# Experts of a two-layer trunk: small work as a list of jobs, one per weight chunk, and the norm's gains multiplied into h by GpSimd

## The chip, the cores and the metric

One Trainium2 chip, one core. The metric is the device time of one execution in microseconds (us). The kernel before has a median of 1207.54 us over three runs, from 1207.18 to 1208.95.

## The reference, cut to what matters

256 tokens with 1024 features go through two layers. Each has a mixer (convolutions and gated linear attention) and a feed-forward part: dense in the first layer, experts in the second. The change lies in the second layer's experts.

```python
def _moe(h, w_router, w_g, w_u, w_d):
    t = h.reshape(-1, D)
    logits = (t @ w_router).astype(jnp.float32)
    top_v, top_i = lax.top_k(logits, TOP_K)
    top_w = jax.nn.softmax(top_v, axis=-1)
    gates = jnp.sum(jax.nn.one_hot(top_i, N_EXPERTS) * top_w[..., None], axis=1)
    for e in range(N_EXPERTS):
        out = out + gates[:, e:e + 1] * ((silu(t @ w_g[e]) * (t @ w_u[e])) @ w_d[e])

f = _rmsnorm(h, ffn_norm_g[layer])
h = h + _moe(f, moe_w_router[j], moe_w_gate[j], moe_w_up[j], moe_w_down[j])
```

The hidden width is 2816, and all is float32.

## The kernel before

Every matmul runs on a fast float32 format with fewer bits, so each operand is split into a high and a low half. `split` (L122) lets ACT copy the high half r (L123) and lets DVE subtract it from the source to get the low half l (L125); with a per-row factor, DVE scales and subtracts in one operation (L127). A product is three matmuls (`mm3`, L182 to L184).

The weights come in chunks of 1 MB, 128 partitions by 2048. `weights` (L135) loads one over SP's queue into a ring (`w`, `wx`, and while the experts run also `e2` and `gy`), and splits it into `wr` and `wl`, every fourth time into `wrx` and `wlx` of another pool. So four split chunks have room, and a chunk can be split only when TensorE has used up the one four before it.

`moe` (L644) first adds the mixer's result to h (L653), transposes h for the router's logits, and splits h into `xr` and `xl` (`xt`), tokens on the partitions. Router and top 2 follow, and for every token and expert a place in that expert's list. The eight experts, ordered by load, form four pairs. The even expert of a pair has up to 128 tokens, the odd one ("few") up to 64. `marks` (L779) builds one-hot matrices of the places on DVE. `pick` (L792) gathers a pair's tokens, by matmuls of `xr` and `xl` with these, into a PSUM bank `gb` for two feature tiles at a time, and splits the result into `xg`, tile by tile and expert by expert, with the norm's gain of the tile's features as the scale. `factors` (L818) gathers gate and norm per row, `back` (L831) makes the transposed one-hot matrix for the way back.

The work of an expert is six items, each a gate and an up projection (`proj`), a transpose of the activations (`turn`, or `fold` and `unfold` for the few expert) and a down projection (`lower`, `down`). Results are scaled (`scale`, L939) and added to h (`finish`, L947). The order is written out by hand. A loop over j (L982) appends steps and chunks to the list `prog`: item j of the even experts, and with a lag of two that of the odd ones. Router places and limits are one step at j = 1; the next pair's pick comes in two lumps at the last item of a pair, factors and back right behind; `extras` puts in pieces of scale and finish. Then `in_order` issues the list: before chunk k runs on TensorE, the loads and splits of all chunks to k + 3 are issued.

```python
        fetch(AHEAD)
        k = 0
        with in_order():
            for wanted, fn in prog:
                if wanted is None:
                    fn()
                    continue
                fetch(k + 1 + AHEAD)
                fn(*ready[k])
                k += 1
```

TensorE, ACT and DVE each keep the order of that list.

Of the kernel before, what the change touches and what calls it, by code (L numbers as in the profile page):

```python
# [17 lines left out]
P = 128  # L18
# [27 lines left out]
NCONST = K_TRI + 128  # L46


def small_arrays(i):
    import numpy as np  # L50
    c = np.zeros((P, NCONST), np.float32)
    rows = [i[n].reshape(-1, P) for n in ("attn_norm_g", "ffn_norm_g", "sc_conv_w", "cf_conv_b", "cf_ln_g",
                                          "cf_ln_b", "gla_norm_g", "cf_conv_w")]
# [57 lines left out]
def trunk_kernel(ctx: ExitStack, tc: tile.TileContext, x, w_in, w_out, dense_w_gate, dense_w_up, dense_w_down,  # L111
# [115 lines left out]
    def late_consts():  # L227
        nc.gpsimd.dma_start(wa2, decay_w)
        stg = tmp([P, 11 + NL, P], "stg", tag="E", bufs=1)
        nc.gpsimd.dma_start(stg, consts[:, K_M:].rearrange("p (l q) -> p l q", q=P))  # L230
        return stg
# [412 lines left out]
    def moe(l, j, accs):  # L644
        ft = tmp([P, KT, T], "ft", tag="A", bufs=1)
# [4 lines left out]
        for tt in range(TT):  # L650
            for nh in range(2):
                cs = slice(nh * 512, nh * 512 + 512)
                nc.vector.tensor_tensor(h[:, tt, cs], h[:, tt, cs], accs[tt][nh], op=ALU.add)  # L653
                tp = bank([P, 4, P], "tp")
# [3 lines left out]
                last_x = nc.scalar.activation(xr[:, tt, cs], h[:, tt, cs], AF.Copy)  # L658
                low_half = partial(nc.vector.tensor_tensor, xl[:, tt, cs], h[:, tt, cs], xr.bitcast(F32)[:, tt, cs],
# [65 lines left out]
        def places():  # L725
            nb = bank([P, NE], "nb")
            for tt in range(TT):
                nc.tensor.matmul(nb, oner, msk[:, tt], start=(tt == 0), stop=(tt == 1))
            cnt = tmp([P, NE], "cnt", tag="rt_b", bufs=1)
            nc.vector.tensor_copy(cnt, nb)  # L730
            w0 = cmp[:, 0, 0:NE]
            w1 = cmp[:, 1, 0:NE]
            lte = lt.rearrange("p (a b) -> p a b", b=NE)
            mine = cnt[:, :, None].broadcast_to([P, NE, NE])
            nc.vector.tensor_tensor(w0, cnt[:, None, :].broadcast_to([P, NE, NE]), mine, op=ALU.subtract)
            nc.vector.scalar_tensor_tensor(w1, w0, 0.0, lte, op0=ALU.is_equal, op1=ALU.mult)
            nc.vector.scalar_tensor_tensor(w0, w0, 0.0, w1, op0=ALU.is_lt, op1=ALU.add)
            rank = tmp([P, NE], "rank", tag="rt_r", bufs=1)
            nc.vector.tensor_reduce(rank, w0[:, :, 1:NE], axis=AX.X, op=ALU.add)
            nc.vector.memset(rank[:, 0:1], -1.0)  # L740
            to = cmp[:, 1, 0:NE]
            nc.vector.tensor_tensor(to, target[:, :, None].broadcast_to([P, NE, NE]),
                                    rank[:, None, :].broadcast_to([P, NE, NE]), op=ALU.is_equal)
            nc.vector.tensor_tensor(w0, to, iota[:, None, 0:NE].broadcast_to([P, NE, NE]), op=ALU.mult)
            idf = tmp([P, NE], "idf", tag="rt_j", bufs=1)
            nc.vector.tensor_reduce(idf, w0, axis=AX.X, op=ALU.add)
            nc.vector.tensor_scalar(ids, idf, -1.0, None, op0=ALU.add)
            for tt in range(TT):
                for src, dst in ((pos[:, tt], placed[:, tt]), (gr[:, tt, :, 0], gp[:, tt, :, 0])):
                    nc.vector.tensor_tensor(w0, to, src[:, None, :].broadcast_to([P, NE, NE]), op=ALU.mult)  # L750
                    nc.vector.tensor_reduce(dst, w0, axis=AX.X, op=ALU.add)
            nc.vector.tensor_copy(gp[:, :, :, 1], rs[:, :, None].broadcast_to([P, TT, NE]))
            nc.vector.tensor_tensor(folded, ident[:, 0:FEW], ident[:, FEW:P], op=ALU.add)
            return cnt, rank

        def limits(cnt, rank):
            few = tmp([P, NE], "few", tag="rt_k2", bufs=1)
            room = tmp([P, NE], "room", tag="rt_r2", bufs=1)
            nc.vector.tensor_scalar(few, rank, -0.5, None, op0=ALU.is_gt)
            nc.vector.scalar_tensor_tensor(few, rank, 3.5, few, op0=ALU.is_lt, op1=ALU.mult)  # L760
            nc.vector.tensor_scalar(room, few, float(FEW - P), float(P), op0=ALU.mult, op1=ALU.add)
            nc.vector.tensor_tensor(over, pos, room[:, None, :].broadcast_to([P, TT, NE]), op=ALU.subtract)
            nc.vector.tensor_tensor(few, cnt, room, op=ALU.subtract)
            nc.vector.tensor_scalar(few, few, 0.0, None, op0=ALU.max)
            nc.vector.tensor_reduce(nmax, few, axis=AX.X, op=ALU.max)
# [13 lines left out]
        def marks(p, i):  # L779
            oh = X[p][1]  # L780
            src = pos if p == 0 and i == 0 else placed
            for tt in range(TT):
# [60 lines left out]

        def chunk(e, src, n, a, b, fn):
            prog.append(((e, src, n, a, b), fn))

# [100 lines left out]
        def finish(e, tts):  # L947
            pt = X[e // 2][3]
            for tt in tts:
                for nh in range(2):  # L950
# [12 lines left out]
        def lower(it):  # L963
# [8 lines left out]
        later = []  # L972

        def extras():
            if later:
                q = later[0]
                step(*q.pop(0))
                if not q:
                    later.pop(0)

        n_pairs = len(items[0]) + LAG
        for j in range(n_pairs + 2):  # L982
            hv, hv1 = item(0, j), item(0, j - 1)
            lt_, lt1, lt2 = (item(1, j - LAG - d) for d in range(3))
            p = j // 6
# [17 lines left out]
            if j == 1:  # L1003
                step(marks, 0, 1)
                step(pick, 0, P, P + FEW)
            if j % 6 == 5 and p + 1 < NE // 2:
                step(pick, p + 1, 0, P + FEW, (0, 1))
            extras()
            if lt_:
                step(proj(0, *lt_))  # L1010
            if j == 1:
                step(factors, 0, 1)
                step(back, 0)
            if j % 6 == 5 and p + 1 < NE // 2:
# [4 lines left out]
            extras()  # L1019
            lower(hv1)  # L1020
            if hv:
                step(turn, *hv)
            extras()
# [4 lines left out]
            if j % 6 == 4 and p + 1 < NE // 2:  # L1028
                step(space, p + 1)
                step(marks, p + 1, 0)  # L1030
                step(marks, p + 1, 1)
            extras()
        while later:
            extras()
# [33 lines left out]
        def rest():  # L1068
            with tc.For_i(0, NE, 1) as ev:
# [11 lines left out]
                for k4 in range(2):  # L1081
                    b = bank([P, 4, P], "gb2")
                    for i in range(4):
# [7 lines left out]
                        nc.scalar.activation(x2[:, kt], b[:, i], AF.Copy, scale=col(R_FFN + KT * l + kt))  # L1091
# [113 lines left out]
```

## Time and profile before

| what | before |
|---|---|
| median of 3 runs | 1207.54 us |
| profiled execution | 1209.62 us, span 1207.8 us |
| mean granted TensorE clock | 0.969 |
| TensorE (PE) busy | 1144.5 us, 95% |
| VectorE (DVE) busy | 1000.0 us, 83% |
| ScalarE (ACT) busy | 802.7 us, 66% |
| GpSimd (POOL) busy | 20.3 us, 2% |
| moved by DMA | 348.46 MB, mean 288 GB/s |

The span is what the profiler saw of the core; the execution's own time is 1.8 us longer. A busy share counts the time in which an engine had an instruction running. The granted clock is 1.00 at TensorE's full level (2.4 GHz), and 0.5 at the lower one (1.2 GHz). In the rows below, "L801" is line 801 of the kernel before, and names such as xg or gb are the kernel's tiles.

### The profile page before, as it was taken

The numbers are of one execution on the slowest core, as the hardware profiler recorded it, in microseconds if no ns is written. First come the engines' busy times: TensorE is split into PE (matmuls) and PEld (weight loads), VectorE is DVE, ScalarE is ACT, GpSimd is POOL, SyncE is SP. The second block draws the span as 40 slices with busy tenths as digits, with TensorE's granted clock in tenths as the row PEclk, the third lists the DMA queues.
The fourth block names the chain that finished last, engine by engine and source line by source line (L and its number), as shares of the span: only waits on it lengthen the run. The fifth ranks groups of instructions, "written<-read, shape, count | busy, mean of one in ns | idle before, by whom it ended". The sixth has DMA issues, their size and how long they took to land.

```text
span 1207.8 us, 17210 instructions
## 1 busy us (share of the span) xinstructions
PE 1144.5 (95%) x6633; PEld 1000.4 (83%) x6633; DVE 1000.0 (83%) x1097; ACT 802.7 (66%) x833; POOL 20.3 (2%) x31
## 2 busy tenths in 40 slices
PE   7999999999899987999889999989999979999996
PEld 6998999999799875888778888868888868888875
DVE  5987755555589767699879999879999979999996
ACT  5644543444465455588778888778788778788874
POOL 2000000000000100000000000000000000000000
PEclk9999999999999979799989999989999989999998
DMA  9344454454333562798979999969999969999991
GB/s 370 122 159 168 168 188 175 177 205 162 139 123 122 235 272 99 295 383 304 381 286 400 398 424 386 403 258 402 389 424 385 425 241 397 387 423 409 424 398 37
DMA packets 48791, 348.46 MB, mean 288 GB/s; under 512 B 5431, under 2 KB 5431, under 8 KB 6976
## 3 DMA queue, kind: packets, MB, share of 16 engines
q1 hardware_dynamic: 48384, 345.50, 72.7%
q0 software_dynamic: 320, 1.80, 0.4%
q8 instruction: 54, 0.88, 0.3%
q14 instruction: 33, 0.27, 0.1%
HBM read 346.23 MB, written 1.05 MB: 288 GB/s over the span
## 4 chain that ended last, share of the span: by engine, by line
PE 90%; DVE 5%; ACT 2%; issue 2%; DMA 0%; POOL 0%; POOLq 0%; SPq 0%; DVEq 0%; ACTq 0%
PE gu L182 10%; PE gu L184 10%; PE gu L183 10%; PE acc_y L182 6%; PE acc_y L183 6%; PE acc_y L184 6%; PE gu L865 6%; PE gu L866 6%; PE acc_y L934 3%; PE acc_y L935 3%; PE fb L907 3%; DVE wl L125 2%; PE gb L801 2%; PE sbk L441 1%; PE a_ps L189 1%
## 5 line engine op out<-in xcount | busy, mean ns | idle before, releaser
L125 DVE TENSOR_TENSOR wl<-w,wr 128x2048 fp32r<-128x2048 f32 (+2 forms) x267 | 464.6, 1762 | 72.3 <-ACT wr L123 72.0
L123 ACT ACTIVATE wr<-w 128x2048 fp32r<-128x2048 f32 (+2 forms) x267 | 392.3, 1490 | 189.9 <-issue 114.4
L125 DVE TENSOR_TENSOR wl<-wx,wr 128x2048 fp32r<-128x2048 f32 x54 | 122.6, 2284 | 10.1 <-ACT wr L123 10.0
L182 PE MATMUL gu<-wr,xg 128*128 128x512 f32 (+1 forms) x296 | 112.2, 379 | 0.0
L184 PE MATMUL gu<-wr,xg 128*128 128x512 f32 (+1 forms) x296 | 111.2, 376 | 0.0
L183 PE MATMUL gu<-wl,xg 128*128 128x512 f32 (+1 forms) x296 | 111.1, 375 | 0.0
L125 DVE TENSOR_TENSOR wlx<-w,wrx 128x2048 fp32r<-128x2048 f32 x45 | 102.8, 2284 | 7.0 <-ACT wrx L123 7.0
L123 ACT ACTIVATE wr<-wx 128x2048 fp32r<-128x2048 f32 x54 | 102.4, 1911 | 7.3 <-PE gu L184 3.8
L865 PE MATMUL gu<-wr,xg 128*128 128x512 f32 (+1 forms) x288 | 106.9, 378 | 0.0
L866 PE MATMUL gu<-wl,xg 128*128 128x512 f32 (+1 forms) x288 | 105.5, 373 | 0.0
L182 PE MATMUL gu<-f,wr 128*128 128x256 f32 x336 | 95.1, 283 | 0.0
L183 PE MATMUL gu<-f,wr 128*128 128x256 f32 x336 | 95.0, 283 | 0.0
L184 PE MATMUL gu<-f,wl 128*128 128x256 f32 x336 | 95.0, 283 | 0.0
L182 PE MATMUL acc_y<-wr,hr 128*128 128x512 f32 x228 | 93.0, 408 | 0.0
L183 PE MATMUL acc_y<-wl,hr 128*128 128x512 f32 x228 | 92.0, 403 | 0.0
L184 PE MATMUL acc_y<-wr,hl 128*128 128x512 f32 x228 | 91.6, 402 | 0.0
L123 ACT ACTIVATE wrx<-w 128x2048 fp32r<-128x2048 f32 x45 | 86.2, 1917 | 3.5 <-DVE wl L125 1.6
L184 PEld LDWEIGHTS gu<-wr,xg 128*128 128x128 f32 x296 | 56.3, 190 | 10.5
L182 PEld LDWEIGHTS gu<-wr,xg 128*128 128x128 f32 x296 | 56.6, 191 | 10.1
L183 PEld LDWEIGHTS gu<-wl,xg 128*128 128x128 f32 x296 | 56.4, 190 | 10.2
L183 PEld LDWEIGHTS gu<-f,wr 128*128 128x128 f32 x336 | 64.4, 192 | 0.4
L182 PEld LDWEIGHTS gu<-f,wr 128*128 128x128 f32 x336 | 64.4, 192 | 0.4
(339 smaller groups left out, 2438.7 us busy)
## 6 DMA issues: line engine op xcount, KB each, us to landing
w<-in_moe_w_gate_dram SPq DMA_DIRECT2D x64, 1024.0 KB, 7.8
w<-in_moe_w_up_dram SPq DMA_DIRECT2D x60, 1024.0 KB, 7.8
w<-in_moe_w_down_dram SPq DMA_DIRECT2D x59, 1024.0 KB, 7.7
wx<-in_moe_w_down_dram SPq DMA_DIRECT2D x25, 1024.0 KB, 7.9
wx<-in_moe_w_gate_dram SPq DMA_DIRECT2D x24, 1024.0 KB, 7.6
wx<-in_moe_w_up_dram SPq DMA_DIRECT2D x23, 1024.0 KB, 7.4
w<-in_w_in_dram SPq DMA_DIRECT2D x20, 1024.0 KB, 4.7
w<-in_dense_w_gate_dram SPq DMA_DIRECT2D x11, 1024.0 KB, 4.9
```

Source lines behind the costliest of these rows:

```text
L123: i0 = nc.scalar.activation(r, src, AF.Copy, scale=scale)
L125: i1 = nc.vector.tensor_tensor(l, src, r.bitcast(F32), op=ALU.subtract)
L182: nc.tensor.matmul(o, sr, mr, start=start, stop=False)
L183: nc.tensor.matmul(o, sr, ml, start=False, stop=False)
L184: nc.tensor.matmul(o, sl, mr, start=False, stop=stop)
L189: nc.tensor.matmul(o, s[:, kt], m[:, kt], start=(n == 0 and kt == 0), stop=(n == 2 and kt == KT - 1))
L801: nc.tensor.matmul(b[:, i, c0:c1], xs[:, tt, kt * P:(kt + 1) * P], oh[:, tt].rearrange("p a b -> p (a b)")[:, c0:c1], start=(n == 0), stop ...
L865: nc.tensor.matmul(o, xg[:, 2, kt], wr[:, i], start=(kt == 0), stop=False)
L866: nc.tensor.matmul(o, xg[:, 2, kt], wl[:, i], start=False, stop=(kt == KT - 1))
L907: nc.tensor.matmul(b[:, n, i], kept[n][:, i * P:(i + 1) * P], X[e // 2][4], start=True, stop=True)
L934: nc.tensor.matmul(Y[e][nh], hb, wr[:, i, cs], start=first, stop=False)
L935: nc.tensor.matmul(Y[e][nh], hb, wl[:, i, cs], start=False, stop=fin)
```

## The change

- **Jobs.** A list `jobs` holds small tasks; `chunk` takes one from it behind each weight chunk. The router's `places` becomes six functions (count, order, assign, where, shares, limits). marks, factors, back and every pick of two feature tiles are one job each, scale two and finish four. `collect` queues a pair's jobs: pair 1 at j = 4, the others when the odd expert two pairs earlier is through. Before the first item of a new pair, picks that are left are issued at once. `extras` is gone, and the turn of item 0 stands behind the first projection of item 1.
- **Gains.** A row of the norm's gains is added to the constants (K_GAIN). `moe` loads it to all partitions, 128x1024, over POOL's queue; POOL multiplies h by it into `hg`, four times 128x512, and `xr` and `xl` are split from hg. hg shares a tile `fh` with the transposed `ft`.
- **Evictions.** A pick's split takes both feature tiles at once, 128x256 for the even expert and 128x2x64 for the few one, without a scale.

```diff
 def moe(l, j, accs):
-        ft = tmp([P, KT, T], "ft", tag="A", bufs=1)
+        gains = mix.tile([P, D], F32, name="gains")
+        nc.gpsimd.dma_start(gains, bass.AP(tensor=consts.tensor, offset=consts.offset + K_GAIN, ap=[[0, P], [1, D]]))
+        fh = tmp([P, 2, KT * T], "fh", tag="A", bufs=1)
...
                 nc.vector.tensor_tensor(h[:, tt, cs], h[:, tt, cs], accs[tt][nh], op=ALU.add)
+                nc.gpsimd.tensor_tensor(hg[:, tt, cs], h[:, tt, cs], gains[:, cs], op=ALU.mult)
...
-                last_x = nc.scalar.activation(xr[:, tt, cs], h[:, tt, cs], AF.Copy)
-                low_half = partial(nc.vector.tensor_tensor, xl[:, tt, cs], h[:, tt, cs], xr.bitcast(F32)[:, tt, cs],
+                last_x = nc.scalar.activation(xr[:, tt, cs], hg[:, tt, cs], AF.Copy)
+                low_half = partial(nc.vector.tensor_tensor, xl[:, tt, cs], hg[:, tt, cs], xr.bitcast(F32)[:, tt, cs],
...
-                for i in range(2):
-                    kt = 2 * k2 + i
-                    gain = col(R_FFN + KT * l + kt)
-                    if c0 == 0:
-                        split(b[:, i, 0:P], xg[:, 0, kt], xg[:, 1, kt], scale=gain)
-                    if c1 > P:
-                        split(b[:, i, P:P + FEW], xg[:, 2, kt, 0:FEW], xg[:, 2, kt, FEW:P], scale=gain)
+                ks = slice(2 * k2, 2 * k2 + 2)
+                if c0 == 0:
+                    split(b[:, :, 0:P], xg[:, 0, ks], xg[:, 1, ks])
+                if c1 > P:
+                    split(b[:, :, P:P + FEW], xg[:, 2, ks, 0:FEW], xg[:, 2, ks, FEW:P])
...
+        jobs = []
+
         def chunk(e, src, n, a, b, fn):
             prog.append(((e, src, n, a, b), fn))
+            if jobs:
+                step(*jobs.pop(0))
...
-                later.append([(scale, e, (0,)), (scale, e, (1,)), (finish, e, (0,)), (finish, e, (1,))])
+                jobs.extend([(scale, e, (0,)), (scale, e, (1,))])
+                jobs.extend((finish, e, (tt,), (nh,)) for nh in range(2) for tt in range(TT))
+                if e % 2 == 1 and e < NE - 3:
+                    collect(e // 2 + 2)
+
+        def collect(p):
+            jobs.extend([(space, p), (marks, p, 0), (marks, p, 1)])
+            jobs.extend([(factors, p, 0), (factors, p, 1), (back, p)])
+            jobs.extend((pick, p, 0, P + FEW, (k2,)) for k2 in range(KT // 2))
+
+        jobs.extend((fn,) for fn in places())
+        jobs.extend([(marks, 0, 1), (factors, 0, 1), (back, 0)])
+        jobs.extend((pick, 0, P, P + FEW, (k2,)) for k2 in range(KT // 2))
...
+            if j == 4:
+                collect(1)
+            if hv and hv[1] == 0 and j:
+                while any(job[0] is pick for job in jobs):
+                    step(*jobs.pop(0))
...
             if j == 1:
-                step(lambda: limits(*places()))
-            extras()
+                step(turn, *hv1)
...
-                step(pick, p + 1, 0, P + FEW, (0, 1))
...
-                step(pick, p + 1, 0, P + FEW, (2, 3))
-                for i in range(2):
-                    step(factors, p + 1, i)
-                step(back, p + 1)
```

How the order moves is seen on three engines. First DVE behind the first gather. Before, from the turn of item 0 (hl) to the first few-expert gather, with the router's placement (L730 to L765, 27 operations in all) between two weight splits:

```order
L125 TENSOR_TENSOR hl_4609<-tb_4603,hr_4608 128x512
L125 TENSOR_TENSOR wlx_4614<-e2_4411,wrx_4613 128x2048
L125 TENSOR_TENSOR wl_4632<-e2_4411,wr_4631 128x2048
L730 COPY cnt_4652<-nb_4649 128x8
L735 TENSOR_TENSOR cmp_4413<-cnt_4652 128x64
L736 SCALAR_TENSOR_TENSOR cmp_4413<-cmp_4413,kc_73 128x64
L737 SCALAR_TENSOR_TENSOR cmp_4413<-cmp_4413 128x64
L739 TENSOR_REDUCE rank_4657<-cmp_4413 128x8
L740 MEMSET rank_4657 128x1
L742 TENSOR_TENSOR cmp_4413<-kc_73,rank_4657 128x64
L744 TENSOR_TENSOR cmp_4413<-cmp_4413,kc_73 128x64
L746 TENSOR_REDUCE idf_4662<-cmp_4413 128x8
```

The same engine after the change:

```order
L744 COPY cnt_4441<-nb_4543 128x8
L127 TENSOR_TENSOR wl_4550<-w_4547,wr_4549 128x2048
L749 TENSOR_TENSOR cmp_4419<-cnt_4441 128x64
L750 SCALAR_TENSOR_TENSOR cmp_4419<-cmp_4419,kc_73 128x64
L751 SCALAR_TENSOR_TENSOR cmp_4419<-cmp_4419 128x64
L752 TENSOR_REDUCE rank_4442<-cmp_4419 128x8
L753 MEMSET rank_4442 128x1
L843 COPY rg_4573<-rgb_4570 128x2
L127 TENSOR_TENSOR wl_4580<-wx_4577,wr_4579 128x2048
L756 TENSOR_TENSOR cmp_4419<-kc_73,rank_4442 128x64
L758 TENSOR_TENSOR cmp_4419<-cmp_4419,kc_73 128x64
L759 TENSOR_REDUCE idf_4443<-cmp_4419 128x8
```

The placement now begins before the second split of the projections, and a group of it stands behind each split.

Second, ACT at a gather for a whole pair. Before, the first lump of eight evictions (xg) and what follows:

```order
L123 ACTIVATE xg_5444<-gb_5557,kc_73 128x128
L123 ACTIVATE xg_5444<-gb_5557,kc_73 128x64
L123 ACTIVATE xg_5444<-gb_5557,kc_73 128x128
L123 ACTIVATE xg_5444<-gb_5557,kc_73 128x64
L123 ACTIVATE xg_5444<-gb_5574,kc_73 128x128
L123 ACTIVATE xg_5444<-gb_5574,kc_73 128x64
L123 ACTIVATE xg_5444<-gb_5574,kc_73 128x128
L123 ACTIVATE xg_5444<-gb_5574,kc_73 128x64
L123 ACTIVATE wr_5593<-wx_5591 128x2048
L123 ACTIVATE wr_5608<-wx_5606 128x2048
L876 ACTIVATE kept_5620<-gu_5597 128x512
```

After the change, at the third pair:

```order
L125 ACTIVATE wrx_6741<-w_6739 128x2048
L125 ACTIVATE xg_6616<-gb_6758 128x256
L125 ACTIVATE xg_6616<-gb_6758 128x2x64
L125 ACTIVATE wr_6773<-w_6771 128x2048
L125 ACTIVATE xg_6616<-gb_6789 128x256
L125 ACTIVATE xg_6616<-gb_6789 128x2x64
L125 ACTIVATE wr_6805<-wx_6803 128x2048
L125 ACTIVATE xg_6616<-gb_6818 128x256
L125 ACTIVATE xg_6616<-gb_6818 128x2x64
L125 ACTIVATE wr_6833<-wx_6831 128x2048
L125 ACTIVATE xg_6616<-gb_6845 128x256
```

Two evictions stand between two weight copies, four times; DVE has the same pattern with its subtractions.

Third, POOL's queue at the kernel's start, after the change; before, the row L648 is not there:

```order
L350 MEMSET u_133 128x2x30
L230 DMA wa2_79<-in_decay_w_dram 17x512
L648 DMA gains_4337<-in_consts_dram 128x1024
L260 ISA
L260 TENSOR_TENSOR st_88<-st_88,half_75 128x1
```

The load of the gains stands ahead of POOL's first part of the norm (st).

## Rows read from the trace of the kernel before

**Rows 1.** The page: TensorE's busy time, and the chain that ended last by engine.

```profile
PE 1144.5 (95%) x6633; PEld 1000.4 (83%) x6633; DVE 1000.0 (83%) x1097; ACT 802.7 (66%) x833; POOL 20.3 (2%) x31
...
PE 90%; DVE 5%; ACT 2%; issue 2%; DMA 0%; POOL 0%; POOLq 0%; SPq 0%; DVEq 0%; ACTq 0%
```

**Rows 2.** Stretches: us, PE, PEld, DVE, ACT, POOL busy, clock, DMA share, GB/s.

```profile
455.00:500.00 45.00, 34.91 (x149) 29.53 (x148) 28.16 (x52) 20.59 (x21) 0.00 (x0) 0.81 0.43 167
500.00:597.00 97.00, 97.00 (x487) 81.59 (x486) 90.16 (x58) 77.48 (x60) 0.00 (x0) 1.00 0.93 361
597.00:611.00 14.00, 6.46 (x35) 5.76 (x34) 8.65 (x18) 8.57 (x18) 0.00 (x0) 0.65 0.67 265
611.00:780.00 169.00, 169.00 (x839) 141.95 (x838) 161.78 (x108) 137.68 (x108) 0.00 (x0) 1.00 0.96 389
...
604.40:787.30 182.90, 175.27 (x871) 147.56 (x872) 170.43 (x126) 146.15 (x123) 0.00 (x0) 0.98 0.94 379
```

**Rows 3.** Waits of TensorE from 440 us on: us in total, times, longest.

```profile
PE ptb L836 <- DVE xg L127: 11.1, 3, 3.7
PE rgb L823 <- ACT kept L876: 9.3, 3, 3.1
PE gb L801 <- DVE xg L787: 6.7, 1, 6.7
PE tb L895 <- DVE s L886: 3.4, 1, 3.4
...
PE rgb L823 <- DVE xg L127: 2.3, 3, 0.8
```

**Rows 4.** Chain of waits from 455 to 500 us: start, duration, what.

```profile
464.60 1.11 PE tb L895 x4
...
484.73 7.04 PE gb L801 x32
```

**Rows 5.** Chain of waits around the first boundary, from 597 to 613 us.

```profile
597.57 1.78 PE gb L801 x16
...
608.46 1.09 PE ptb L836 x4
609.55 0.43 PE acc_y L182
...
611.57 0.23 PE acc_y L184
```

**Rows 6.** Groups by form from 424 us on: busy, mean ns of one | idle before.

```profile
L125 DVE TENSOR_TENSOR wl<-wx,wr 128x2048 fp32r<-128x2048 f32 x54 | 122.6, 2284 | 10.1 <-ACT wr L123 10.0
...
L125 DVE TENSOR_TENSOR hl<-tb,hr 128x512 fp32r<-128x512 f32 x20 | 13.6, 681 | 1.8 <-ACT hr L123 1.8
...
L127 DVE SCALAR_TENSOR_TENSOR xg<-gb,kc,xg 128x128 fp32r<-128x128 f32 x32 | 11.1, 349 | 8.7 <-ACT xg L123 8.5
L127 DVE SCALAR_TENSOR_TENSOR xg<-gb,kc,xg 128x64 fp32r<-128x64 f32 x32 | 9.1, 284 | 15.1 <-ACT xg L123 15.1
...
L125 DVE TENSOR_TENSOR wl<-w,wr 128x1024 fp32r<-128x1024 f32 x2 | 2.4, 1216 | 0.0
...
L125 DVE TENSOR_TENSOR hl<-tb,hr 128x256 fp32r<-128x256 f32 x4 | 1.7, 416 | 0.0
...
L123 ACT ACTIVATE wr<-wx 128x2048 fp32r<-128x2048 f32 x54 | 102.4, 1911 | 7.3 <-PE gu L184 3.8 <-PE acc_y L184 1.8 <-ACT wrx L123 0.9
```

**Rows 7.** Timeline of ACT and of DVE at that boundary.

```profile
606.23 0.31 ACT L123 ACTIVATE xg<-gb,kc 128x64 fp32r<-128x64 f32 x1 [2.28 <-DVE xg L127]
...
601.44 4.50 DVE L125 TENSOR_TENSOR wl<-wx,wr 128x2048 fp32r<-128x2048 f32 x2 [1.51 <-ACT wr L123]
```

**Rows 8.** Timeline of POOL, DVE and ACT in the first 27 us.

```profile
22.43 1.79 POOL L237 CAST mk<-stg 128x1024 uint8<-128x1024 f32 x1 [9.24 <-DMA stg<-in_consts_dram]
...
22.09 3.20 DVE L125 TENSOR_TENSOR wl<-w,wr 128x1024 fp32r<-128x1024 f32 x2 [2.54 <-ACT wr L123]
...
9.36 2.00 ACT L123 ACTIVATE wr<-w 128x1024 fp32r<-128x1024 f32 x2 [2.20 <-DMA w<-in_w_in_dram]
```

More of the change, by code (lines that the diff above doesn't have):

```diff
@@ L45 @@
 K_TRI = K_ONE + 128
-NCONST = K_TRI + 128
+K_GAIN = K_TRI + 128
+NCONST = K_GAIN + D
 def small_arrays(i):
@@ L51, in small_arrays @@
     c = np.zeros((P, NCONST), np.float32)
+    c[0, K_GAIN:] = i["ffn_norm_g"][1]
     rows = [i[n].reshape(-1, P) for n in ("attn_norm_g", "ffn_norm_g", "sc_conv_w", "cf_conv_b", "cf_ln_g",
@@ L229, in late_consts @@
         stg = tmp([P, 11 + NL, P], "stg", tag="E", bufs=1)
-        nc.gpsimd.dma_start(stg, consts[:, K_M:].rearrange("p (l q) -> p l q", q=P))
+        nc.gpsimd.dma_start(stg, consts[:, K_M:K_GAIN].rearrange("p (l q) -> p l q", q=P))
         return stg
@@ L644, in moe @@
     def moe(l, j, accs):
-        ft = tmp([P, KT, T], "ft", tag="A", bufs=1)
+        gains = mix.tile([P, D], F32, name="gains")
+        nc.gpsimd.dma_start(gains, bass.AP(tensor=consts.tensor, offset=consts.offset + K_GAIN, ap=[[0, P], [1, D]]))
+        fh = tmp([P, 2, KT * T], "fh", tag="A", bufs=1)
+        ft = fh[:, 0].rearrange("p (k t) -> p k t", k=KT)
+        hg = fh[:, 1].rearrange("p (t d) -> p t d", t=TT)
         xt = tmp([P, 2, TT, D], "xt", tag="Y", bufs=1, dt=F32R)
@@ L725, in places @@
         def places():
[L726 to L730, printed above, removed]
+            cnt, rank, idf, few, room = (tmp([P, NE], n, tag="rt_" + n, bufs=1)
+                                         for n in ("cnt", "rank", "idf", "few", "room"))
             w0 = cmp[:, 0, 0:NE]
             w1 = cmp[:, 1, 0:NE]
-            lte = lt.rearrange("p (a b) -> p a b", b=NE)
@@ L734, in places @@
[L734 to L765, printed above, removed]
+            to = cmp[:, 0, NE:2 * NE]
@@ new lines, in places, with count, order @@
+            V = nc.vector
+            def count():
+                nb = bank([P, NE], "nb")
+                for tt in range(TT):
+                    nc.tensor.matmul(nb, oner, msk[:, tt], start=(tt == 0), stop=(tt == 1))
+                V.tensor_copy(cnt, nb)
+            def order():
+                lte = lt.rearrange("p (a b) -> p a b", b=NE)
+                mine = cnt[:, :, None].broadcast_to([P, NE, NE])
+                V.tensor_tensor(w0, cnt[:, None, :].broadcast_to([P, NE, NE]), mine, op=ALU.subtract)
+                V.scalar_tensor_tensor(w1, w0, 0.0, lte, op0=ALU.is_equal, op1=ALU.mult)
+                V.scalar_tensor_tensor(w0, w0, 0.0, w1, op0=ALU.is_lt, op1=ALU.add)
+                V.tensor_reduce(rank, w0[:, :, 1:NE], axis=AX.X, op=ALU.add)
+                V.memset(rank[:, 0:1], -1.0)
@@ new lines, in assign, with move @@
+            def assign():
+                V.tensor_tensor(to, target[:, :, None].broadcast_to([P, NE, NE]),
+                                rank[:, None, :].broadcast_to([P, NE, NE]), op=ALU.is_equal)
+                V.tensor_tensor(w0, to, iota[:, None, 0:NE].broadcast_to([P, NE, NE]), op=ALU.mult)
+                V.tensor_reduce(idf, w0, axis=AX.X, op=ALU.add)
+                V.tensor_scalar(ids, idf, -1.0, None, op0=ALU.add)
+            def move(tt, src, dst):
+                V.tensor_tensor(w0, to, src[:, None, :].broadcast_to([P, NE, NE]), op=ALU.mult)
+                V.tensor_reduce(dst, w0, axis=AX.X, op=ALU.add)
@@ new lines, in where, with shares, limits @@
+            def where():
+                for tt in range(TT):
+                    move(tt, pos[:, tt], placed[:, tt])
+            def shares():
+                for tt in range(TT):
+                    move(tt, gr[:, tt, :, 0], gp[:, tt, :, 0])
+                V.tensor_copy(gp[:, :, :, 1], rs[:, :, None].broadcast_to([P, TT, NE]))
+                V.tensor_tensor(folded, ident[:, 0:FEW], ident[:, FEW:P], op=ALU.add)
+            def limits():
+                V.tensor_scalar(few, rank, -0.5, None, op0=ALU.is_gt)
+                V.scalar_tensor_tensor(few, rank, 3.5, few, op0=ALU.is_lt, op1=ALU.mult)
+                V.tensor_scalar(room, few, float(FEW - P), float(P), op0=ALU.mult, op1=ALU.add)
+                V.tensor_tensor(over, pos, room[:, None, :].broadcast_to([P, TT, NE]), op=ALU.subtract)
+                V.tensor_tensor(few, cnt, room, op=ALU.subtract)
+                V.tensor_scalar(few, few, 0.0, None, op0=ALU.max)
+                V.tensor_reduce(nmax, few, axis=AX.X, op=ALU.max)
@@ L767, in moe @@
+            return count, order, assign, where, shares, limits
         gw, uw, dw = moe_w_gate[j], moe_w_up[j], moe_w_down[j]
@@ L777, in block, with marks @@
             return src[bass.ds(expert[p], 1), n].rearrange("e p n -> (e p) n")
-        def marks(p, i):
+        def marks(p, i, tts=range(TT)):
             oh = X[p][1]
             src = pos if p == 0 and i == 0 else placed
-            for tt in range(TT):
+            for tt in tts:
                 e = 2 * p + i
@@ L945, in scale, with finish @@
             return last
-        def finish(e, tts):
+        def finish(e, tts, nhs=(0, 1)):
             pt = X[e // 2][3]
             for tt in tts:
-                for nh in range(2):
+                for nh in nhs:
                     cb = bank([P, 512], "cb")
@@ L969, in lower @@
             if c == 5 and e < NE - 1:
-                later.append([(scale, e, (0,)), (scale, e, (1,)), (finish, e, (0,)), (finish, e, (1,))])
[L972 to L979, printed above, removed]
+                jobs.extend([(scale, e, (0,)), (scale, e, (1,))])
[9 more added lines that the diff above has]
+        jobs.extend((pick, 0, P, P + FEW, (k2,)) for k2 in range(KT // 2))
         n_pairs = len(items[0]) + LAG
@@ L1002, in moe @@
                 step(proj(1, *hv))
[L1003 to L1006, printed above, removed]
-                step(pick, p + 1, 0, P + FEW, (0, 1))
-            extras()
             if lt_:
                 step(proj(0, *lt_))
[L1011 to L1014, printed above, removed]
-                step(pick, p + 1, 0, P + FEW, (2, 3))
-                for i in range(2):
-                    step(factors, p + 1, i)
-                step(back, p + 1)
-            extras()
             lower(hv1)
-            if hv:
+            if hv and j:
                 step(turn, *hv)
-            extras()
             if lt_:
@@ L1027, in moe @@
                 lower(lt2)
[L1028 to L1034, printed above, removed]
+        for job in jobs:
+            step(*job)
         queue = [q[0] for q in prog if q[0] is not None]
@@ L1090, in rest @@
                                 n += 1
-                        nc.scalar.activation(x2[:, kt], b[:, i], AF.Copy, scale=col(R_FFN + KT * l + kt))
+                        nc.scalar.activation(x2[:, kt], b[:, i], AF.Copy)
                 b = bank([P, T], "ptb2")
```

1 line of the change is left out of this document (removed).

## The prediction

> **What bounds the kernel now.** I began with the page's busy shares and the chain of waits. TensorE is busy 95% of the span and is 90% of the chain that ended last [rows 1], so time is to be had only where TensorE stands still or runs at its lower clock. Next, a table by stretches of the experts' part [rows 2]. From 500 to 597 and from 611 to 780 us TensorE is busy without a gap at the full granted clock (97.00 of 97.00, 169.00 of 169.00): nothing the change does there can show. Two kinds of stretch are different: the **start** of the experts (455 to 500 us: 34.91 of 45 busy, clock 0.81) and a **boundary between two pairs** (597 to 611 us: 6.46 of 14, clock 0.65). The third view, TensorE's waits from 440 us on, says what ended them [rows 3]. At the start the gather of the few expert waits 6.7 us for its one-hot marks and the turn of item 0 waits 3.4 us for DVE's product s, 10.1 us in all. The boundary comes three times, and its waits add up to 11.1 + 9.3 + 2.3 = 22.7 us, 7.6 us each: for an eviction (xg) on DVE, or for a copy (kept) on ACT which stands behind the evictions.
>
> Behind each wait TensorE runs at the 1.2 GHz level for a while. At the start 32 gather matmuls took 7.04 us and the four transposes of item 0 took 1.11 us [rows 4]; in the gap-free stretch ahead of a boundary 16 wider gather matmuls took 1.78 us [rows 5], so 32 should take 3.56. A 512-column matmul takes 0.43 us behind a wait and 0.23 us otherwise [rows 5]; nine of them stand behind the two waits of the start, and at least four behind each boundary.
>
> **The change, part by part.**
>
> *Jobs at the start.* 27 small DVE operations of the router stood in one lump between two weight splits. They now stand in groups of up to seven, one group behind each chunk; the turn of item 0 moves behind item 1's first projection, and the second gather comes in four pieces. No DVE work disappears. What TensorE loses in 455 to 500 us today is 10.1 us of waiting, 3.5 us in the slow gather, half of 1.11 in the slow transposes, and nine matmuls by 0.20 (1.8): about 16 us. Its work without these is 29 us. DVE is busy 28.16 us in the same stretch [rows 2], so it just keeps up, but it has to deliver a split every 2.28 us [rows 6] with the groups between them, each of which TensorE may meet. Following the new order by hand I find waits of 1.0, 0.5 and about 0.5 us left: 31 us in place of 45, a **gain of 14 us**. The bounds: 16 if nothing is left, 3 if the lump only changes into many short waits that keep the clock low. I take 14, because TensorE keeps work in reserve: one chunk's products stand between the marks and the first instruction that needs them, and the gather comes two chunks later still.
>
> *Collections at the boundaries.* Before, sixteen evictions on each engine came in two lumps of eight. Within a lump ACT and DVE take turns, since they go to the same PSUM bank: ACT's next eviction waits for DVE's last one, 2.28 us where DVE still has a split ahead of it [rows 7]. Two splits of DVE, 4.50 us, stand between the lumps [rows 7]. Now one group of two feature tiles is gathered behind each of four chunks, and its evictions are two operations on each engine in place of four. Their price: DVE's 128x128 form with the gain took 0.349 us and its 128x64 form 0.284 [rows 6]; the new 128x256 has a row of its own in hl, 0.416, and for the new 128x2x64 I take the 0.35 of the 128x128 form. DVE per pair: 8 x 0.349 + 8 x 0.284 = 5.1 becomes 4 x (0.416 + 0.35) = 3.1, so 2.0 us less. That by itself is hidden (DVE is busy 170.43 of 182.90 us per pair [rows 2]).
>
> What decides is the cycle. The second eviction on ACT still waits for DVE's first one (one bank). Behind it ACT makes the high half of the next chunk (1.91), then DVE the low half (2.28) [rows 6], then DVE's first eviction (0.42), then ACT's second (0.3): with the hand-overs about 5.1 us per gather chunk. TensorE needs 8 or 12 matmuls by 0.23 and half of 1.78 for the gather: 2.8 to 3.7 us. Four such chunks run late by 6 to 9 us in all. Chunks are split three ahead: at best TensorE has three chunks of some 2.6 us in hand when the first late one takes 1.91 + 2.28, a reserve of up to 3.6 us. So 4 to 7 us are still lost at each boundary, where it is 7.6 us of waiting and about 2 at the low clock now. I take 5.5 lost, a gain of 4 each, **12 us for three**. The bounds are nothing, and all 28.
>
> *Gains multiplied by GpSimd.* POOL takes four products of 128x512 in the chain that ends in the first gather, and ACT's and DVE's halves of x wait for them. No POOL product of that size stands in the trace. The nearest rows: a POOL cast of 128x1024 took 1.79 us [rows 8], twice the elements with one input; DVE's two-input form of the same size, hl of 128x512, took 0.681 [rows 6]. Between them I take 1.2 us. Router and logits do not go through it: they hang on h and its transposes. But ACT's copies for the logits stand in one queue with the halves. Beside the cast, two DVE operations of 128x1024 took 3.20 us [rows 8] where each takes 1.216 [rows 6]: a loss of 0.8 us. Against this, the marks of the first expert now stand ahead of two weight splits on DVE, which saves up to 0.8 us. I take **0.6 us lost**, bounds -0.4 and 2.
>
> The Trainium skill, in SBUF — State Buffer, Who interferes with whom, says that a VectorE instruction with two SBUF inputs and a GpSimd instruction that reads SBUF exclude each other, whichever starts second standing fully blocked. The 3.20 us beside the cast agree with a block. By that rule alone each of the four products could hold a DVE operation for its whole length, 4.8 us in all by my 1.2; I don't take this, since VectorE's row of that stretch also waits for ACT and TensorE, which hides a part.
>
> *Gains loaded at the start.* A new broadcast of 512 KB goes out on POOL's queue in the first microseconds, when the first weight copy on ACT waits 2.20 us for its DMA [rows 8]. At the 389 GB/s of rows 2 it costs at most 1.3 us; at least nothing. I take **0.8 us lost**, as all queues share the same engines. Its place among POOL's instructions has a second effect: later chunks' memory overlaps it, and two loads wait until POOL has read it; TensorE has enough loaded chunks there, so nothing.
>
> The turn of item 0, the finish in four steps and the rest beyond 977 us move within gap-free stretches: nothing.
>
> **Sum.** -14 - 12 + 0.6 + 0.8 = -24.6. The profiled execution took 1209.62 us (span 1207.8), 2.1 above the median 1207.54. So 1185.0 against it, **1183** as a median.
>
> **Rivals.**
>
> 1. *The boundaries vanish wholly* (the reserve covers all four gathers). For it: the evictions are spread over four chunks. Against it: DVE would have 168 of 173 us to work, and the weights' DMA, whose share is 0.94 over a pair at 379 GB/s [rows 2], would need 0.99. 1209.6 - 14 - 28 + 1.4 = 1169, as a median 1167. Chance 0.13.
> 2. *Only one half pays.* Either the evictions at a boundary still take turns with splits between them, and the loss stays 9.5 us: 1209.6 - 14 + 1.4, as a median 1195. Or the start gains only its lower bound, 3: 1209.6 - 3 - 12 + 1.4, as a median 1194. For it: in the new order a weight split now stands between every two evictions, so each of them can be as late as a split is. Chance 0.21.
> 3. *Slower: TensorE fed in pieces drops to 1.2 GHz and stays there.* At a boundary it now gets four pieces of 3 us, one every 5.1 us, where it had two long waits. At the low level a gather chunk takes 5.6 to 7.4 us, more than the 5.1 of its feeders, so TensorE itself becomes the bound; should it stay there for six chunks, it loses about 6 x 2.8 + 3 = 20 us per boundary, 10 more than now. 1209.6 - 14 + 1.4 + 30 = 1227, as a median 1225. It decides if the granted clock over such a stretch falls below about 0.6. Against it: before, the full level was back after four slow matmuls [rows 5]. Chance 0.05.
> 4. *The change does not do what it says*: the jobs run, but the same waits come under other names, and all ends within 0.2% (2.4 us, about what a measurement of this kernel can tell from no change). Chance 0.03.
>
> **How the numbers follow.** The forecast has 0.58. It and rivals 1 and 2 are all faster by more than 0.2%, together 0.92; the same 0.03; slower 0.05. The range goes from a little below rival 1 (both bounds of the start on top of it) to a little above rival 2: 1163 to 1198. What is left out are rivals 3 and 4 and the tails.
>
> **What the next profile would show.** Right: no wait of the gather for marks (6.7) and the gather at the full level; in 455 to 490 us TensorE idle under 3 us; at each boundary several waits of 1 to 2 us for splits or evictions in place of two of 3 to 4, with a granted clock above 0.8; POOL with four products of 1 to 1.5 us near 428 to 436 us; the first weight copy on ACT up to a microsecond later. Wrong: waits of TensorE at the boundaries still over 7 us each (rival 2), a gap-free boundary (rival 1), rows of 0.43 us over a dozen matmuls behind each gather (rival 3), or an end of the router that is more than 2 us later than today, from POOL's products.

## The result and the profile after

The changed kernel takes **1186.52 us** (median of 4 runs, 1185.49 to 1187.54), against 1208.24 for the kernel before: ratio 0.9819, 95% interval 0.9805 to 0.9832. The forecast was 1183, the range 1163 to 1198. So the medians differ by 21.7 us. The profiled execution took 1185.49 us with a span of 1183.5, so 24.1 us less than the one of before; the sum had 24.6. The profile of before fell on a long execution (1209.62 us), this one on the shortest of four, which brings the two figures nearer. "L841" is now line 841 of the kernel after; the kernels of the experiments have lines of their own.

The page of the kernel after, busy times and chain by engine, answers to [rows 1]:

```profile
PE 1138.0 (96%) x6633; PEld 992.4 (84%) x6633; DVE 990.5 (84%) x1065; ACT 789.5 (67%) x801; POOL 28.0 (2%) x36
...
PE 80%; DVE 10%; issue 4%; ACT 4%; DMA 1%; POOL 0%; SPq 0%; POOLq 0%; DVEq 0%; ACTq 0%
```

TensorE runs 6633 matmuls as before. They keep it busy for 6.5 us less (1138.0 for 1144.5), since fewer of them stand at the low level; the rest of the gain is time in which it stood still. DVE's share of the chain doubled from 5 to 10%. That is not more waiting of TensorE, which is busy for 96% of the span and has only 80% of the chain: around a boundary the chain now runs over DVE and ACT while TensorE still works on chunks in hand. The stretches after (columns as in [rows 2]), and one of before that is as wide:

```profile
457.00:490.00 33.00, 28.94 (x134) 23.40 (x133) 27.30 (x44) 19.62 (x16) 0.00 (x0) 0.95 0.64 246
490.00:560.00 70.00, 70.00 (x344) 58.51 (x343) 62.49 (x46) 54.96 (x42) 0.00 (x0) 1.00 0.87 329
560.00:600.00 40.00, 37.66 (x205) 32.35 (x204) 32.16 (x26) 29.50 (x30) 0.00 (x0) 0.96 0.79 298
600.00:740.00 140.00, 140.00 (x686) 117.10 (x685) 136.33 (x94) 113.79 (x89) 0.00 (x0) 1.00 1.01 412
740.00:790.00 50.00, 46.31 (x235) 38.60 (x234) 43.28 (x30) 38.72 (x34) 0.00 (x0) 0.97 0.86 327
930.00:970.00 40.00, 36.27 (x193) 30.08 (x191) 37.66 (x24) 33.93 (x27) 0.00 (x0) 1.00 0.91 359
```

```profile
750.00:800.00 50.00, 42.37 (x230) 36.65 (x229) 41.06 (x44) 34.69 (x39) 0.00 (x0) 0.90 0.80 326
```

At the start the granted clock is 0.95, where it was 0.81. Around the three boundaries it is 0.96, 0.97 and 1.00, where the second one had 0.90 in a stretch of 50 us before. TensorE stands still there for 2.3, 3.7 and 3.7 us, where it was 7.5 of 14 at the first one [rows 2] and 7.6 at the second. The stretches between are gap-free as before. TensorE's waits from 430 us on (us in all, times, longest) answer to [rows 3]:

```profile
PE rgb L841 <- DVE xg L807: 3.6, 1, 3.6
PE gu L888 <- DVE wl L127: 3.3, 3, 1.8
PE acc_y L956 <- DVE hb L127: 2.4, 1, 2.4
PE gu L185 <- DVE wl L127: 2.1, 2, 1.9
PE gu L888 <- DVE wlx L127: 1.8, 1, 1.8
```

The waits for evictions and for kept at the boundaries, 22.7 us in all, are gone. In their place stand waits for weight splits (wl, wlx). One new wait stands in the tail: 2.4 us for hb (the few expert's split activations) of the last item. And 3.6 us for the few expert's marks are left at the start, where the forecast had no more than 1; they now hold up the gather of its factors (rgb), not of its tokens.

How a boundary looks now is read from ACT's and DVE's timelines at the second one:

```profile
745.19 0.37 ACT L125 ACTIVATE xg<-gb 128x256 fp32r<-128x256 f32 x1
747.98 0.28 ACT L125 ACTIVATE xg<-gb 128x128 fp32r<-128x128 f32 x1 [2.42 <-DVE xg L127]
748.33 1.91 ACT L125 ACTIVATE wr<-wx 128x2048 fp32r<-128x2048 f32 x1
750.14 0.37 ACT L125 ACTIVATE xg<-gb 128x256 fp32r<-128x256 f32 x1
...
745.32 2.29 DVE L127 TENSOR_TENSOR wl<-wx,wr 128x2048 fp32r<-128x2048 f32 x1 [0.85 <-ACT wr L125]
747.53 0.41 DVE L127 TENSOR_TENSOR xg<-gb,xg 128x256 fp32r<-128x256 f32 x1
748.29 0.29 DVE L127 TENSOR_TENSOR xg<-gb,xg 128x128 fp32r<-128x128 f32 x1 [0.34 <-ACT xg L125]
750.27 2.29 DVE L127 TENSOR_TENSOR wl<-wx,wr 128x2048 fp32r<-128x2048 f32 x1 [1.69 <-ACT wr L125]
```

This is the cycle of the forecast. ACT's second eviction (747.98) begins 0.04 us after DVE's first one ends (747.94), which stands behind DVE's split; ACT's next weight copy stands behind the eviction, and DVE's next split behind that copy. From one first eviction to the next (745.19 to 750.14) it takes 4.95 us; the forecast had 5.1. The Trainium skill, in PSUM — Partial Sum Buffer, PSUM bank collisions raise a hardware error, states that two engines must not be at one PSUM bank at the same time; the 0.04 us agree with accesses put in series for that.

### The profile page after: what moved, and what is told of

Read it like the earlier page. It is cut to its first block, busy times and chain, and to the rows that moved or that the text cites. A ratio compares the mean times of both kernels' runs of the same rounds, so it can differ in the third digit from the quotient of the medians.

```text
span 1183.5 us, 17163 instructions
## 1 busy us (share of the span) xinstructions
PE 1138.0 (96%) x6633; PEld 992.4 (84%) x6633; DVE 990.5 (84%) x1065; ACT 789.5 (67%) x801; POOL 28.0 (2%) x36
## 4 chain that ended last, share of the span: by engine, by line
PE 80%; DVE 10%; issue 4%; ACT 4%; DMA 1%; POOL 0%; SPq 0%; POOLq 0%; DVEq 0%; ACTq 0%
PE gu L184 9%; PE gu L185 9%; PE gu L186 9%; PE acc_y L184 6%; PE acc_y L185 6%; PE acc_y L186 6%; DVE wl L127 5%; PE gu L888 5%; PE gu L887 5%; PE fb L929 3%; PE acc_y L956 3%; PE acc_y L957 2%; ACT wr L125 2%; DVE wlx L127 2%; PE sbk L443 1%
## 5 line engine op out<-in xcount | busy, mean ns | idle before, releaser
L185 PEld LDWEIGHTS gu<-wl,xg 128*128 128x128 f32 x296 | 57.1, 193 | 12.6 <-DVE wl L127 2.6
L888 PEld LDWEIGHTS gu<-wl,xg 128*128 128x128 f32 x288 | 54.3, 189 | 13.0 <-DVE wl L127 4.3
L185 PEld LDWEIGHTS gu<-f,wr 128*128 128x128 f32 x336 | 64.4, 192 | 0.4
```

Of the source, the lines that this page charges most:

```text
L185: nc.tensor.matmul(o, sr, ml, start=False, stop=False)
L888: nc.tensor.matmul(o, xg[:, 2, kt], wl[:, i], start=False, stop=(kt == KT - 1))
```

## The experiments

Each edit is made alone to the kernel after the change, to be compared with its 1186.52, where nothing else is said. The kernel before, run beside these, had medians from 1208.99 to 1209.73 us, where it had 1208.24 beside the changed one. So a difference of under some 1.5 us is not told apart from none.

**The gains loaded later.** The load waits in POOL's queue behind the last norm of the second mixer.

```diff
-        nc.gpsimd.dma_start(gains, ...)
+        with behind((area["power"],)):
+            nc.gpsimd.dma_start(gains, ...)
```

> The load of the gains goes out behind the last norm of the second mixer (about 320 us) instead of in the first 3 us; all else as after the change. Theory (the 512 KB stand ahead of the first weights on the same DMA engines): the first split of a weight on ACT starts about 2.0 us earlier, at 9.3 in place of 11.4 us, the whole kernel becomes 2 to 3 us faster, 1183.5 to 1184.5, and nothing is given back at 320 us. Rival (the first 440 us are longer for another reason, such as the wider row of constants): first weight copy still near 11.4 us, time 1186 to 1187.

Measured 1182.89 us (1181.74 to 1183.37), 3.6 less. The first weight copy on ACT, in the kernel after and with the late load:

```profile
11.40 2.00 ACT L125 ACTIVATE wr<-w 128x1024 fp32r<-128x1024 f32 x2 [4.08 <-DMA w<-in_w_in_dram]
```

```profile
9.44 2.00 ACT L125 ACTIVATE wr<-w 128x1024 fp32r<-128x1024 f32 x2 [2.24 <-DMA w<-in_w_in_dram]
```

Its wait for the DMA was 2.20 us before the change [rows 8], 4.08 after it, and is 2.24 with the late load. The theory holds: the load cost 2.0 us at once, and in these two traces 2.4 us by the first logit (436.57 against 434.13 us); nothing is given back at 320 us. The 3.6 us of the medians are a little more than was expected.

**ACT's evictions first.** Same instructions, another order.

```diff
-                if c0 == 0:
-                    split(b[:, :, 0:P], xg[:, 0, ks], xg[:, 1, ks])
...
+                for s, r, _ in todo:
+                    nc.scalar.activation(r, s, AF.Copy)
+                for s, r, low in todo:
+                    nc.vector.tensor_tensor(low, s, r.bitcast(F32), op=ALU.subtract)
```

> In a pick's eviction ACT writes both high halves before DVE subtracts either, so that ACT's second eviction no longer waits for DVE's first one (it did for 2.42 us, twice per boundary in the trace after the change). Theory (cycle of weight copy, weight split, eviction on DVE, eviction on ACT, 4.95 us per pick, is what TensorE waits for at the boundaries): cycle falls to some 3.0 us, TensorE's waits at the three boundaries fall from 2.3, 3.7 and 3.6 us to under 1 each, and the time by 6 to 8 us, 1178 to 1180. Rival A (weights' DMA or DVE's own work is the bound there): the waits move to a DMA or stay, gain under 3 us. Rival B (the even and the few expert's evictions contend for the bank): ACT's and DVE's evictions grow longer, no gain.

Measured 1169.94 us (1169.74 to 1172.46): 16.6 less, twice what was expected. ACT's timeline and the stretch of the second boundary:

```profile
739.22 0.55 ACT L832 ACTIVATE xg<-gb 128x256 fp32r<-128x256 f32 x2 [0.39 <-PE gb L821]
739.66 1.92 ACT L125 ACTIVATE wr<-wx 128x2048 fp32r<-128x2048 f32 x1
741.97 0.55 ACT L832 ACTIVATE xg<-gb 128x256 fp32r<-128x256 f32 x2 [0.39 <-PE gb L821]
...
740.00:765.00 25.00, 25.00 (x147) 21.92 (x146) 23.00 (x17) 21.39 (x19) 0.00 (x0) 1.00 0.97 360
```

The two evictions stand together, the cycle is 2.75 us (739.22 to 741.97), and ACT now waits for TensorE's gather. TensorE has no gap at any boundary. Rival A falls: DVE (23.00 of 25 us) and the DMA (0.97) still had room. So does rival B: ACT's two evictions take 0.55 us together, no longer than apart (0.37 and 0.28). The size was off in the main because only the waits were counted, 9.8 us in all. Behind the wait of 1.8 us in the kernel after, the chain has matmuls at the low level:

```profile
757.87 0.79 PE gu L888
758.66 0.43 PE gu L887
...
761.22 0.18 PE gu L184
```

Seven matmuls there took 3.35 us (757.87 to 761.22) in place of 1.6. At the first boundary narrower ones did so, at the third none. The profiled executions differ by 13.0 us; the rest of the 16.6 is not accounted for.

**limits behind the few expert's gather.** The job of seven small DVE operations goes from ahead of the marks to the end of the first list.

> The job limits (7 small DVE operations) goes from ahead of the few expert's marks to the end of the first list. Theory (TensorE's 3.6 us wait for the marks at 476 us is one of order on DVE): marks come 3 to 4 us earlier, the wait vanishes with the matmuls of 0.43 us behind it, 3 to 5 us faster, 1181.5 to 1183.5. Rival (DVE is full there, 27.3 of 33 us, so that another wait for DVE takes its place): gain under 1.5 us, with a new wait for hl or a weight split of 2 us or more in the same place.

Measured 1184.11 us, but from 1180.61 to 1187.25, so its size is unsure. The marks (L807) on DVE in the kernel after, and with the edit:

```profile
477.04 2.28 DVE L127 TENSOR_TENSOR wl<-gy,wr 128x2048 fp32r<-128x2048 f32 x1
479.23 0.48 DVE L807 TENSOR_SCALAR xg<-kc,placed 128x128 fp32r<-128x128 f32 x2
```

```profile
474.45 0.48 DVE L807 TENSOR_SCALAR xg<-kc,placed 128x128 fp32r<-128x128 f32 x2
...
475.44 2.28 DVE L127 TENSOR_TENSOR wl<-gy,wr 128x2048 fp32r<-128x2048 f32 x1
```

The marks come 4.8 us earlier, 0.7 of them by an earlier first gather: neither limits nor that split stands ahead of them now. But with one job fewer in the list their user on TensorE also moved up by one chunk, so the wait fell only from 3.6 to 2.4 us. From the first gather to that of the second pair it takes 115.7 us in place of 118.6: the place itself gained 2.9 us in this trace, near the theory. The profiled execution lost them again behind, where the edit moves nothing, with a mean clock of 0.981 for 0.985. The rival's new wait did not come.

**Additions of expert 6 behind the last hb.**

> The four additions of expert 6's result to h are made behind the last item's hb, their matmuls stay where they are. Theory (spread one behind each of the last weight splits, they hold up s and hb of the last item, for which TensorE waits 2.4 us): hb comes 2 to 2.5 us earlier, the wait falls under 0.5, the time by 1.5 to 2.5 us, 1184 to 1185. Rival (the additions then delay the last yg and the final norm by as much, since DVE has only 2.0 us free there): no change, within 0.5 us of 1186.5.

Measured 1183.55 us (1182.62 to 1185.08), 3.0 less, a little more than expected. The wait for hb fell from 2.4 to 0.5 us, and the four additions find room on DVE just ahead of the last yg (the scaled result):

```profile
1167.05 0.29 DVE L127 TENSOR_TENSOR hb<-s,hb 128x128 fp32r<-128x128 f32 x1 [0.38 <-ACT hb L125]
1167.26 2.47 DVE L973 TENSOR_TENSOR h<-h,cb 128x512 f32<-128x512 f32 x4
1169.65 1.40 DVE L129 SCALAR_TENSOR_TENSOR yg<-acc_y,rg,yg 128x512 fp32r<-128x512 f32 x2
```

**The jobs alone.** Gains, load and two-tile evictions are taken back.

> The jobs alone: POOL's product, the load of the gains and the two-tile evictions are taken back, a pick evicts tile by tile with the gain as scale. Theory (what TensorE waits for at a boundary is a cycle in series over ACT and DVE; four evictions per engine in place of two make it about 1.5 us longer, 6.5 in place of 4.95): each boundary loses some 5 us more, the load's 3.5 us are not paid, 1194 to 1203. Rival (the number of evictions does not matter, they hide behind the splits): 1182 to 1185.

Measured 1206.59 us (1204.40 to 1207.89), ratio to the kernel before 0.9978 (0.9967 to 0.9988). So the jobs by themselves bring almost nothing, less than the theory's range; the rival is far off. ACT at the second boundary:

```profile
754.69 0.36 ACT L125 ACTIVATE xg<-gb,kc 128x128 fp32r<-128x128 f32 x1
757.41 0.32 ACT L125 ACTIVATE xg<-gb,kc 128x64 fp32r<-128x64 f32 x1 [2.37 <-DVE xg L129]
...
760.88 0.36 ACT L125 ACTIVATE xg<-gb,kc 128x128 fp32r<-128x128 f32 x1
```

The cycle is 6.19 us (754.69 to 760.88) in place of 4.95, as four evictions per engine take turns. TensorE's waits at the three boundaries come to 20.7 us, so nearly the 22.7 of before, and the tail has the new wait of 2.4 us for hb. Where the rest of what the start wins is lost was not followed.

**The gains alone**, in the order of the kernel before.

> The other half alone: gains by POOL and two-tile evictions in the order of the kernel before, without jobs. Theory: the start keeps its 10.1 us of waits; at each boundary a lump has four evictions in turn in place of eight, some 2.5 us less each, of which TensorE's waits give back 2 to 4 us per boundary; the load costs 3. Sum 1208 - 9 + 2: 1199 to 1204. Rival (the lumps' length does not matter, only the splits between them): 1208 to 1211, slower than before by the load.

Measured 1199.05 us (1197.48 to 1199.80), ratio 0.9917 (0.9900 to 0.9933): the theory, at its lower end. TensorE's waits from 440 us on:

```profile
PE ptb L841 <- DVE xg L127: 8.1, 3, 2.7
PE gb L808 <- DVE xg L794: 6.8, 1, 6.8
PE rgb L828 <- ACT kept L881: 3.8, 3, 1.3
PE tb L900 <- DVE s L891: 3.4, 1, 3.4
```

The start's 6.8 and 3.4 are those of [rows 3]; the boundaries' waits fell from 22.7 to 11.9. Together the two halves bring 21.7 us (1208.24 to 1186.52); alone about 2.5 and 10 by their own comparisons. Some 9 us are had only by both. The cycles of 6.19 and 4.95 us say why: spread picks need short evictions.

**The first expert's factors ahead of the first projection.**

> After the change, with the first expert's factors (two small matmuls and a copy on DVE) ahead of the first projection instead of behind it. Theory (in the trace after the change ACT's silu of item 0 waits 2.2 us for that copy, which stands behind a weight split and a job on DVE; the weight copies behind it come late, DVE then waits 2.6 us, and the marks of the few expert come late by as much): DVE's wait near 460 us falls under 1, TensorE's wait for the marks from 3.6 to 1 to 2 us, 2 to 4 us faster, 1182.5 to 1184.5. Rival (order of the marks on DVE alone decides): no change of the 3.6 us, 1186 to 1187.

Measured 1185.47 us (1183.56 to 1186.58), about 1 less, which is within the spread. The split near 460 us, which waited 2.56 us in the kernel after (shown below), with the edit:

```profile
461.68 2.29 DVE L127 TENSOR_TENSOR wl<-wx,wr 128x2048 fp32r<-128x2048 f32 x1 [0.49 <-ACT wr L125]
```

So the theory's first step holds, ACT's silu waits for no copy any more. The wait for the marks fell to 2.6, less than the theory has it; the time followed by no more than that.

**The gains multiplied by DVE.**

> The kernel after the change with the four products of h and the gains on DVE instead of POOL. In the trace after the change POOL's four products took 7.87 us from start to end, 1.97 each, and the low halves of x on DVE beside them 0.89 to 1.08 us in place of 0.68. Theory (the products stand in the chain to the first gather only where ACT or DVE is idle anyway, so the engine matters little): DVE does them in 0.7 each, its own chain grows by 2.8 less the 1 us that the halves win back; first gather 0 to 1.5 us later, time 1186 to 1188.5. Rival (POOL's slow products hold up the chain): the first gather comes over 1 us earlier, 1184 to 1185.5.

Measured 1192.91 us (1191.67 to 1194.33): 6.4 slower, outside both. With its additions later on DVE, the last group of transposes waits 2.08 us, and the logits behind it run at the lower clock (granted 0.50, in the kernel after 1.00); TensorE with DVE's product, and then in the kernel after:

```profile
436.88 0.80 PE L663 MATMUL tp<-kc,h 128*128 128x128 f32 x4 [2.08 <-DVE rs L681]
437.47 6.84 PE L673 MATMUL lb<-wrg,fh 128*128 128x8 f32 x32
```

```profile
434.83 1.91 PE L663 MATMUL tp<-kc,h 128*128 128x128 f32 x16
436.57 3.64 PE L673 MATMUL lb<-wrg,fh 128*128 128x8 f32 x32
```

So 3.2 us are lost in 32 tiny matmuls by the clock and 2.1 by the wait. Another 1.0 is lost at the first gather, as the marks stand behind half a weight split here:

```profile
PE gb L821 <- DVE xg L805: 1.6, 1, 1.6
```

In the kernel after that wait is 0.6. The three make 6.3 us, near the 6.4; taking the products off DVE was worth more than POOL's slowness costs.

**All four edits together**, and with the factors first as a fifth.

> The four edits tried alone before (late load of the gains, ACT's evictions first, limits last, additions of expert 6 behind the last hb) in one kernel. Theory (four separate places, each with its own wait): the gains add up, 16.6 + 3.6 + 2.4 + 3.0 us off 1186.5, 1160 to 1163. Rival (the weights' DMA or DVE becomes the bound once the boundaries are gap-free): the sum stops short, 1165 or more, with TensorE waiting for splits or loads elsewhere.

> The four edits together and the first expert's factors ahead of the first projection. Theory (the marks of the few expert, for which TensorE still waits 2.4 us at 468 us, come late by the sum of what stands ahead of them on ACT and DVE): that wait falls by about 1 us as it did for this edit alone (3.6 to 2.6), 1158 to 1159.5. Rival (with limits out of the way the two edits remove the same microsecond): 1159.5 to 1161.

Measured 1159.74 us (1159.23 to 1161.92) with four, ratio to the kernel before 0.9599 (0.9583 to 0.9615), and 1160.04 (1158.78 to 1161.35) with five, ratio 0.9592 (0.9578 to 0.9605). The four add up by the medians: 25.6 us singly, 26.8 together. In both traces, though, the first logit comes at 430.5 and 430.9 us, over 3 us earlier than with the late load alone (434.1), and what brings that is open; so the sum is no proof for each part. The fifth shortens the marks' wait to 1.3 us and brings no time that can be told. Both beat the kernel before and the changed one. With four, TensorE is busy for 549.96 of 550 us from 560 to 1110, with a DMA share of 1.00:

```profile
560.00:1110.00 550.00, 549.96 (x2770) 463.18 (x2768) 532.07 (x359) 455.05 (x362) 0.63 (x1) 1.00 1.00 403
```

## Why the prediction was right, and where its steps were off

The forecast of the total, 24.6 for 24.1 us, is nearer than its parts, and that is luck in good part: the start was set down some 4 us too high and the boundaries some 4 too low, and POOL's products and the load were off by 1.6 and about 2 in opposite directions.

- **The boundaries** (forecast 12 us gained, 5.5 lost at each). The mechanism holds: same cycle, 4.95 for 5.1. What is left came to 16.6 us by the medians, 13.0 by the profiled executions, when the order of ACT's evictions removed it, where 3 x 5.5 = 16.5 had been set down. The gain itself is larger than 12. Of the 24.1 us between the profiled executions, about 10 come from the start and 1.0 from the router, the first logits come 3.0 later, and the tail gives nothing: some 16 are left for the boundaries. The loss before was sized too small: the "about 2 at the low clock" came from the first boundary alone, where four matmuls of 0.43 us stand [rows 5]. Behind the second there are seven (792 to 795 us), behind the third nine (976 to 980).
- **The start** (forecast 14) was sized too large. TensorE still waits 3.6 us for the marks and 0.4 for s, and seven matmuls of 0.43 follow (481.53 to 484.52 us); with the 0.20 lost in each that is 5.4 us left, not 2, so about 10 gained of the 16. TensorE is idle for 4.1 of 33 us, where the forecast's sign was under 3. The step that failed is the walk through the new order: it let DVE go from split to split. But ACT's silu (s) waits 2.2 us for a copy on DVE (rg) that stands behind a split and four small operations, and the weight copies behind it make DVE wait 2.6 us:

```profile
460.40 0.69 ACT L904 ACTIVATE s<-gu,rg 128x512 f32<-128x512 f32 x1 [2.16 <-DVE rg L843]
```

```profile
456.98 2.29 DVE L127 TENSOR_TENSOR wl<-w,wr 128x2048 fp32r<-128x2048 f32 x1 [1.66 <-ACT wr L125]
...
460.21 0.15 DVE L843 COPY rg<-rgb 128x2 f32<-128x2 f32 x1
...
462.92 2.29 DVE L127 TENSOR_TENSOR wl<-wx,wr 128x2048 fp32r<-128x2048 f32 x1 [2.56 <-ACT wr L125]
```

  Taking limits out of the way and putting the factors first shortened the wait for the marks, to 2.4 and 2.6 alone and 1.3 together, as such a chain would have it.
- **The gains' load** (0.8, bound 1.3): 2.0 us at the first weight copy, 2.4 at the first logit, 3.6 in the medians. The bound was wrong: 512 KB by the steady rate is not what a load costs that stands ahead of the first weights. Its own landing took 9.5 us.
- **POOL's products** (0.6 lost): from the first logit to the first gather it took 7.81 us before and 6.80 after, so 1.0 gained. The four products took 3.29, 1.27, 1.72 and 1.71 us; only the second is near the 1.2 taken. The first one started beside a weight split on DVE that kept its usual time (timelines of POOL and DVE after the change):

```profile
431.60 3.29 POOL L660 TENSOR_TENSOR fh<-h,gains 128x512 f32<-128x512 f32 x1 [20.76 <-DVE h L659]
...
431.44 2.29 DVE L127 TENSOR_TENSOR wl<-w,wr 128x2048 fp32r<-128x2048 f32 x1
```

  The split ended at 433.73 us and the product 1.16 us later. The Trainium skill's rule (SBUF — State Buffer, Who interferes with whom) agrees: the second to start stood until the first was done. That the stretch became shorter all the same is the marks, which now stand ahead of two split halves: the first gather waits 0.6 us for them, where it was 1.6 before. The other runs bear it out. With the gains alone the wait is 0.6 and the stretch 6.76 us; with the jobs alone, where POOL has no product, they are 1.6 and 7.81. So the products themselves cost nothing that shows there.
- **The tail** was priced at nothing; it got a new wait of 2.4 us for hb and lost most of those for yg, so the sum is right by two errors. The stretch beyond 977 us was not gap-free before:

```profile
PE cb L953 <- DVE yg L127: 3.0, 2, 2.7
```

- **The rivals.** The boundaries did not vanish, nor did only one half pay, and TensorE did not stay at the low level: 0.96 and more around a boundary.

## What to carry to other kernels

When two engines empty one PSUM bank, issue all operations of the first engine before those of the second; one after the other in pairs ties the first engine's queue to the second one's, and all that stands behind it. A small task that is moved into another engine's queue is paid for by what stands next in that queue: look for who waits for it, above all at the last item, where no work is left to hide it. And a load that is needed late should be issued late, even if its queue is idle.

## What was not expected of the hardware

- 32 matmuls of 8 columns took 6.84 us behind a wait of 2.08 us and 3.64 without it, so 1.9 times as long, like 512 columns with 0.43 for 0.23: the granted level weighs as much on tiny matmuls as on large ones. The granted clock was 0.50 from 437.5 to 444.3 us, so no return to the full level was seen within that stretch.
- A load of 512 KB broadcast from one row took 9.5 us to land among the first weights, and 4.1 us at 320 us.
